# One weight transfer with eight rows a partition, a strided on-chip turn, and four transfers held back by a copy count

## The chip, the cores and the metric

The kernel runs on one core of a Trainium2 chip. A core has a matrix engine (TensorE, in the profile PE for the matrix products and PEld for its weight loads), a vector engine (VectorE, DVE), a scalar engine (ScalarE, ACT), a general engine (GpSimd, POOL) and a synchronisation engine (SyncE, SP). Each engine runs its own list of instructions and waits on counters called semaphores. Transfers between the device memory and the on-chip memory are issued by an engine and carried out by 16 DMA engines. The on-chip memory has 128 partitions.

The metric is the device time of one execution in microseconds (us). The kernel before takes 206.82 us, the median of three runs (206.81 to 207.0).

## The reference

The inputs are x of 16 x 512 x 1024, a weight of 1024 x 768, the number scale = 0.1, and add_value of 16 x 512 x 768, all in float32. What is computed is

```python
def reference(x, weight, scale, add_value):
    return (scale * np.matmul(x, weight) + add_value).astype(np.float32)
```

With the first two dimensions of x put together there are 8192 rows, contraction length K = 1024 and N = 768 columns. The kernel multiplies in bfloat16, accumulates in float32, and adds in float32.

## The kernel before, in words

The 8192 rows are cut into 64 tiles of 128 rows, numbered 0 to 63. In one group of 16 tiles, partition p holds 16 consecutive rows of the matrix, so that a transfer of eight tiles moves one contiguous run a partition: 32768 bytes of x, or 24576 bytes of add_value or of the output.

Five lists of work run side by side, one for each engine.

**SyncE** (`sync_engine`) issues nearly all transfers, in the order of the list `STREAM`. An entry names a kind, a first tile and a number of tiles: `w` is weight, `x` is the input, `a` is add_value, `o` is a store of the output, and `a+` only books the second half of a double load of add_value. The first load of x (tiles 0 to 7) is issued ahead of the list. The buffer `xs` has room for 16 tiles of x, and the buffer `ao` for 32 tiles of add_value, which also becomes the output in place. So before an entry is issued, SyncE waits for what makes its room free: for `x`, that ScalarE (`by_act`) and GpSimd (`by_pool`) have copied the tiles that it overwrites; for `a`, that the load of add_value before it has landed, and that the store that used the slots has landed; for `o`, that VectorE has finished the tiles (`made`) and that the store two before it has landed. SyncE works strictly in this order, so what stands behind a waiting entry waits too. The helper `need` leaves out a wait that an earlier one already covers. `SYNC_AT` names the place in the list at which the instruction stream is aligned; it stands before the entry `("a", 8, 8)` both times.

**ScalarE and GpSimd** (`mover`) copy x from `xs` to one of two buffers `va`, from float32 to bfloat16, four tiles at a time. Such a step of four tiles is called a move; there are 16 moves. In each move each of the two engines makes 8 copies of 32 partitions x 1024 elements, shifting blocks of 32 partitions, and each copy adds one to `by_act` or `by_pool`: after all moves each count stands at 128. Move m may start when its x has landed and when the turns of move m - 2 are done.

**VectorE** (`vector_engine`) first casts the weight to bfloat16 (`cast_w`, two instructions of four of the eight weight slabs each). Then it alternates two kinds of work. `turn` transposes 32 x 32 blocks of half a move (two tiles) from `va` to `xt`, on pairs of bfloat16 values seen as one 4-byte word. `finish` takes the products of two tiles from the accumulator `mm`, scales them and adds add_value in `ao`. Turns 0 and 1 come first; after that each finish of a pair of tiles is followed by the turn of the pair two later.

**TensorE** (`tensor_engine`) takes the tiles in order: eight weight loads a tile, and two products (512 and 256 columns) for each. It works on two tiles for each turn.

**GpSimd** also stores tiles 8 and 15 itself, as three transfers over different partitions (`BY_POOL`), after 64 of its 128 copies.

How the contraction index is dealt out matters for the change. The weight has 1024 rows. Before, slab pair c holds the rows 256 c + 2 p and 256 c + 2 p + 1 on partition p: two consecutive rows, 6144 bytes, are contiguous in the device memory, and each of the two weight transfers moves two such runs a partition. The tiles of x are put in the matching order by the copies (four runs of 64 values for each of four tiles, thus 16 x 64) and by the turn, which reads `va` from end to end.

Of the kernel before, what the change touches and what calls it, by code (L numbers as in the profile page):

```python
# [8 lines left out]
P = 128  # L9
# [7 lines left out]
VA_BUFS = 2  # L17
MOVE = 4
AHEAD = 4
HALF_BLOCK, PAST, SYNC_AT = 64, 4, 4  # L20

STREAM = [
# [6 lines left out]
]  # L29
FIRST, ENDING = (0, 8), 48  # L30
PAIR, TURN_AT = slice(8, 16, 7), 2
BY_POOL = [(122, 6), (0, 98), (98, 24)]

# [2 lines left out]
def kernel(  # L36
# [9 lines left out]
    bf16 = mybir.dt.bfloat16  # L46
    fp32 = mybir.dt.float32
# [7 lines left out]
    KC = K // (2 * P)  # L55
    KJ = 2 * KC
# [1 line left out]
    x_v = x_f.rearrange("(g p t) k -> p g t k", p=P, t=R)  # L58
    add_v = add_f.rearrange("(g p t) n -> p g t n", p=P, t=R)
    out_v = out_f.rearrange("(g p t) n -> p g t n", p=P, t=R)  # L60
    w_v = weight.rearrange("(c p r) n -> p c (r n)", p=P, r=2)

    def rows(view, s, n):
        assert s // R == (s + n - 1) // R
        return view[:, s // R, s % R:s % R + n, :]
# [3 lines left out]
    xs = nc.alloc_sbuf_tensor("xs", [P, X_SLOTS, K], fp32).ap()  # L69
    const = ctx.enter_context(tc.tile_pool(name="const", bufs=1))  # L70
    ao = const.tile([P, A_SLOTS, N], fp32, name="ao")
    w_bf = const.tile([P, KJ, N], bf16, name="w_bf")
    va = [const.tile([P, MOVE * KC, 4, 64], bf16, name=f"va{i}") for i in range(VA_BUFS)]
    xt = const.tile([P, XT_TILES, KC, P], fp32, name="xt")
    mm = psum.tile([P, MM_BUFS, 1024], fp32, name="mm")

    end_sem = nc.alloc_semaphore("ending")
    w_sem = [tc.alloc_semaphore(f"w{i}") for i in range(2)]
    x_sem = [tc.alloc_semaphore(f"x{i}") for i in range(X_SLOTS // MOVE)]
    a_sem = tc.alloc_semaphore("a")  # L80
    o_sem = [tc.alloc_semaphore(f"o{i}") for i in range(2)]
# [1 line left out]
    by_act, by_pool, pool_go, turned, casts, done, made = (  # L83
        tc.alloc_semaphore(name)
        for name in ("by_act", "by_pool", "pool_go", "turned", "casts", "done", "made"))
    TURNED = MOVE * VA_BUFS
    MADE = TURNED + 2 + MM_BUFS - 2
    W_AT = A_SLOTS - KJ

    def slot(t):  # L90
        return t % A_SLOTS
# [5 lines left out]
    def sync_engine(eng):  # L97
        groups, stores, known = 0, [], {}

        def need(sem, value):  # L100
            if known.get(sem, 0) < value:
                eng.wait_ge(sem, value)  # L102
                known[sem] = value

        for at, (op, s, n) in enumerate(STREAM):
            if at == SYNC_AT:
                eng.addr_align(HALF_BLOCK, offset=PAST, max_nops=0)
            last = s + n - 1
            if op == "w":
                dst = ao[:, W_AT + s:W_AT + s + n, :].rearrange("p (c r) n -> p c (r n)", r=2)  # L110
                move, sem = eng.dma_start(dst, w_v[:, s // 2:(s + n) // 2, :]), w_sem[s // 4]
            elif op == "x":
                k = s % X_SLOTS
                if last >= X_SLOTS:
                    moved = 8 * (last + 1 - X_SLOTS) // MOVE
                    need(by_act, moved)
                    need(by_pool, moved)
                move = eng.dma_start(xs[:, k:k + n, :], rows(x_v, s, n))  # L118
                sem = x_sem[k // MOVE]
            elif op == "a":  # L120
                if groups:
                    need(a_sem, 16 * groups)
                if last == A_SLOTS - 1:
                    need(casts, KJ)
                if s <= PAIR.start + A_SLOTS <= last:
                    need(aside_sem, 16 * len(BY_POOL))
                if s >= A_SLOTS:
                    i = next(j for j, (a, b) in enumerate(stores) if a <= last - 1 - A_SLOTS < a + b)
                    need(o_sem[i % 2], 16 * (i // 2 + 1))
                move = eng.dma_start(ao[:, slot(s):slot(s) + n, :], rows(add_v, s, n))  # L130
                sem = a_sem
                groups += 1
            elif op == "a+":
                need(a_sem, 16 * groups)
                eng.sem_inc(a_sem, 16 * (n // G - 1))
                groups += n // G - 1
                continue
            else:
                i = len(stores)
                if i > 1:  # L140
                    need(o_sem[i % 2], 16 * (i // 2))
                need(made, MADE + last + 1)
                move = eng.dma_start(rows(out_v, s, n), ao[:, slot(s):slot(s) + n, :])
                sem = o_sem[i % 2] if s < ENDING else end_sem
                stores.append((s, n))
            move.then_inc(sem, 16)
            if op == "x" and n == 2 * MOVE:
                eng.sem_inc(x_sem[k // MOVE + 1], 16)

    def mover(eng, copy, parity, count, go=None, first=0, turns=T // X_SLOTS):  # L150
        if go is None:
            eng.preload_act_table(mybir.ActivationFunctionType.Copy)  # L152
        with eng.Fori(16 * (first + 1), 16 * (first + turns) + 1, 16) as i:  # L153
            for q in range(X_SLOTS // MOVE):
                eng.wait_ge(x_sem[q], i)
                eng.wait_ge(turned, i + (4 * q - 12) if q < 3 else i)  # L156
                if go is not None:
                    eng.sem_inc(go, 1)  # L158
                k = MOVE * q
                src = xs[:, k:k + MOVE, :].rearrange("p i (c b k) -> p (i c) b k", b=4, k=64)  # L160
                for a in (parity, parity + 2):
                    for b in range(4):
                        copy(va[q % VA_BUFS][32 * b:32 * b + 32, :, a, :],  # L163
                             src[32 * a:32 * a + 32, :, b, :]).then_inc(count, 1)

    def vector_engine(eng):
        ao_g = ao.rearrange("p (g t) n -> p g t n", t=G)

        def cast_w(s, n):
            eng.wait_ge(w_sem[s // 4], 16)  # L170
            eng.tensor_copy(w_bf[:, s:s + n, :], ao[:, W_AT + s:W_AT + s + n, :]).then_inc(casts, n)  # L171

        def turn(move, half, moves=None):
            if half == 0:
                eng.wait_ge(by_act, moves)
                eng.wait_ge(by_pool, moves)  # L176
            q = 2 * half * KC
            eng.transpose(  # L178
                xt[:, 2 * half:2 * half + 2, :, :].rearrange("p i c m -> p (i c m)"),
                va[move % VA_BUFS][:, q:q + 2 * KC, :, :].bitcast(fp32).rearrange("p c a k -> p (c a k)"),  # L180
            ).then_inc(turned, 2)

        def finish(pair, at, products):
            eng.wait_ge(done, products)
            a = ao_g[:, at, 2 * pair:2 * pair + 2, :]
            q = 2 * (pair % 2)
            eng.scalar_tensor_tensor(  # L187
                a, mm[:, q:q + 2, 0:N], float(scale), a,
                op0=mybir.AluOpType.mult, op1=mybir.AluOpType.add).then_inc(made, 2)

        def group(i, at, last):
            eng.wait_ge(a_sem, i)
            for p in range(4):
                finish(p, at, i + (4 * p - 12) if p < 3 else i)
                if p < 2 or not last:
                    turn(1 if p < 2 else 0, p % 2, i + 8 if p == 2 else i)

        cast_w(0, 4)
        cast_w(4, 4)
        turn(0, 0, 8)  # L200
        turn(0, 1)
        with eng.Fori(16, 2 * T, 16) as i:
            group(i, bass.ds((i // 16 + A_SLOTS // G - 1) % (A_SLOTS // G), 1), False)
        s = slot(T - G) // G
        group(2 * T, slice(s, s + 1), True)
# [31 lines left out]
    s, n = FIRST  # L237
# [4 lines left out]
    with tc.tile_critical(no_gpsimd_drain=True):  # L242
        sync_engine(nc.sync)
        mover(nc.scalar, nc.scalar.copy, 0, by_act)
        mover(nc.gpsimd, nc.gpsimd.tensor_copy, 1, by_pool, pool_go, 0, TURN_AT)
        nc.gpsimd.wait_ge(made, MADE + PAIR.stop)
        for p, n in BY_POOL:
            store_pair(nc.gpsimd, p, n)
        nc.gpsimd.addr_align(HALF_BLOCK, offset=PAST, max_nops=0)
        mover(nc.gpsimd, nc.gpsimd.tensor_copy, 1, by_pool, pool_go, TURN_AT, T // X_SLOTS - TURN_AT)  # L250
        vector_engine(nc.vector)
        tensor_engine(nc.tensor)
# [40 lines left out]
```

## Time and profile before

| What | before |
|---|---|
| median of three runs | 206.82 us |
| the profiled execution | 206.85 us |
| its span, first to last instruction | 205.5 us |
| busy: PE, ACT, POOL, DVE | 167.5, 134.7, 137.4, 98.0 us |
| moved by the DMA engines | 87.04 MB, mean 424 GB/s |
| mean granted clock of TensorE | 0.986 |

The span is the time from the first to the last instruction of the profiled execution; 1.35 us of its 206.85 us lie around it. Rows of the trace give a start, a duration, the engine, the line in the code, the operation and, in brackets, how long the engine was idle before and what ended that. An "issue" row on SPq is the moment at which SyncE hands a transfer to the DMA engines; its landing is told as the time from issue to the last byte's completion. Windows give for a stretch of time the busy time of each engine, the granted clock, the mean busy share of the 16 DMA engines and the rate at which they moved data. That share counts a packet where it begins, so short windows can show slightly more than 1.

### The profile page before, as it was taken

How to read it: one execution, taken by the hardware profiler on the slowest of the kernel's cores; microseconds unless marked ns; L12 is line 12 of the kernel's file. 1: busy time of each engine (PE TensorE's matmuls, PEld its weight loads, DVE VectorE, ACT ScalarE, POOL GpSimd, SP SyncE). 2: the span in 40 equal slices, each digit the busy share in tenths (PEclk: the TensorE clock that was granted, in tenths of full speed). 3: DMA queues.
4: the chain of work that ended last, by engine and by line, in shares of the span. 5: the costliest groups of instructions: out<-in, count | busy, mean ns of one | idle time of the engine just before them, and what ended most of it. 6: DMA issues, size and time to landing. Idle time of an engine off the chain costs nothing.

```text
span 205.5 us, 2223 instructions
## 1 busy us (share of the span) xinstructions
PE 167.5 (82%) x1008; PEld 50.4 (25%) x512; DVE 98.0 (48%) x66; ACT 134.7 (66%) x129; POOL 137.4 (67%) x135
## 2 busy tenths in 40 slices
PE   0000099999999999999999999999999997999900
PEld 0000022233322333223332233332333322333200
DVE  0004525537555555465555555555552853455330
ACT  2049980699999906999999059999991099920000
POOL 0049994699999916999999549999992099930000
PEclk9999999999999999999999999999999999999995
DMA  8989999999999899999999999999999999998997
GB/s 287 427 372 438 440 485 408 392 437 459 446 459 459 357 459 408 408 426 413 455 404 450 431 416 464 434 411 421 440 431 415 437 448 421 493 459 364 423 440 304
DMA packets 4065, 87.04 MB, mean 424 GB/s; under 512 B 480, under 2 KB 480, under 8 KB 1120
## 3 DMA queue, kind: packets, MB, share of 16 engines
q1 hardware_dynamic: 3856, 86.25, 98.1%
q0 software_dynamic: 208, 0.79, 0.9%
q14 instruction: 1, 0.01, 0.0%
HBM read 61.87 MB, written 25.17 MB: 424 GB/s over the span
## 4 chain that ended last, share of the span: by engine, by line
DMA 38%; PE 36%; POOL 10%; ACT 5%; issue 4%; DVE 3%; SPq 1%; POOLq 0%; DVEq 0%; ACTq 0%
PE mm L210 36%; DMA out_dram<-ao 22%; DMA xs<-in_x_dram 15%; POOL va L163 9%; ACT va L163 5%; DVE xt L178 2%; DVE ao L187 1%; POOL out_dram L95 1%; SPq L130 0%; SPq L118 0%; DVEq L176 0%; SPq L102 0%; POOLq L156 0%; POOLq L158 0%; POOLq L153 0%
## 5 line engine op out<-in xcount | busy, mean ns | idle before, releaser
L210 PE MATMUL mm<-w_bf,xt 128*128 128x256 bf16 (+1 forms) x1008 | 167.5, 327 | 28.0 <-DVE xt L178 27.1
L163 POOL CAST va<-xs 32x1024 bf16<-32x1024 f32 x128 | 135.2, 1056 | 44.2 <-DMA xs<-in_x_dram 36.8
L163 ACT CAST va<-xs 32x1024 bf16<-32x1024 f32 x128 | 133.4, 1042 | 45.2 <-DMA xs<-in_x_dram 42.2
L187 DVE SCALAR_TENSOR_TENSOR ao<-mm,ao 128x1536 f32 (+1 forms) x32 | 56.2, 1756 | 72.9 <-PE mm L210 68.9
L208 PEld LDWEIGHTS <-xt 128*128 128x128 bf16 x512 | 50.4, 98 | 144.6 <-issue 116.6
L178 DVE STREAM_TRANSPOSE xt<-va 128x1024 f32<-128x1024 f32 x32 | 39.4, 1234 | 8.4 <-POOL va L163 6.3
L171 DVE CAST w_bf<-ao 128x3072 bf16<-128x3072 f32 x2 | 4.5, 2240 | 18.1 <-DMA ao<-in_weight_dram 18.1
L152 ACT ACT_TABLE_LOAD x1 | 1.3, 1283 | 1.3 <-SPq L242 1.3
L95 POOL DMA_DIRECT2D out_dram<-ao x3 | 2.0, 672 | 0.0
L274 POOL MEMSET const-float32-0.0<- 128x1 f32 x1 | 0.1, 98 | 0.2 <-issue 0.2
L274 POOL MEMSET const-bfloat16-1.0<- 128x1 bf16 x1 | 0.1, 101 | 0.0
L274 POOL MEMSET const-float32-1.0<- 128x1 f32 x1 | 0.1, 98 | 0.0
L274 POOL MEMSET const-uint8-127<- 128x1 uint8 x1 | 0.1, 98 | 0.0
## 6 DMA issues: line engine op xcount, KB each, us to landing
xs<-in_x_dram SPq DMA_DIRECT2D x7, 4096.0 KB, 20.9
ao<-in_add_value_dram SPq DMA_DIRECT2D x6, 3072.0 KB, 15.7
out_dram<-ao SPq DMA_DIRECT2D x3, 3072.0 KB, 27.4
ao<-in_add_value_dram SPq DMA_DIRECT2D x1, 6144.0 KB, 24.2
out_dram<-ao SPq DMA_DIRECT2D x1, 6144.0 KB, 31.2
out_dram<-ao SPq DMA_DIRECT2D x1, 4608.0 KB, 14.9
xs<-in_x_dram SPq DMA_DIRECT2D x2, 2048.0 KB, 21.0
ao<-in_weight_dram SPq DMA_DIRECT2D x2, 1536.0 KB, 16.8
```

The lines of the kernel that those rows point to most:

```text
L95: eng.dma_start(out_v[p:p + n, 0, PAIR, :], ao[p:p + n, PAIR, :]).then_inc(aside_sem, 16)
L152: eng.preload_act_table(mybir.ActivationFunctionType.Copy)
L163: copy(va[q % VA_BUFS][32 * b:32 * b + 32, :, a, :], src[32 * a:32 * a + 32, :, b, :]).then_inc(count, 1)
L171: eng.tensor_copy(w_bf[:, s:s + n, :], ao[:, W_AT + s:W_AT + s + n, :]).then_inc(casts, n)
L178: eng.transpose(xt[:, 2 * half:2 * half + 2, :, :].rearrange("p i c m -> p (i c m)"), va[move % VA_BUFS][:, q:q + 2 * KC, :, :].bitcast(fp ...
L187: eng.scalar_tensor_tensor(a, mm[:, q:q + 2, 0:N], float(scale), a, op0=mybir.AluOpType.mult, op1=mybir.AluOpType.add).then_inc(made, 2)
L208: eng.ldweights(x_j, tile_position=(0, 0))
L210: m = eng.add_instruction(mybir.InstMatmult(start_tensor_calc=(j == 0), stop_tensor_calc=(j == KJ - 1), tile_size=(P, P), tile_position=(0 ...
L274: nc = _bacc.Bacc("TRN2", target_bir_lowering=False, num_devices=1)
```

## The change

There are three edits.

1. The weight comes in one transfer. Partition p now gets the eight consecutive rows 8 p to 8 p + 7, which is one run of 24576 bytes. There is one semaphore for it, so both casts wait for the whole weight. SyncE issues one transfer less. `SYNC_AT` goes from 4 to 3, since the list is shorter by one.
2. The order of x has to follow. The copies now move four runs of 256 consecutive values (4 x 256 in place of 16 x 64, still 1024 elements). The turn reads `va` with a step of four 4-byte words between neighbouring elements and writes `xt` from end to end as before.
3. A table `HELD` adds a wait on ScalarE's count `by_act` ahead of four entries of the list: the store of tile 0 on (54 copies), the load of add_value for tile 32 on (66), the store of tile 16 on (92) and the store of tile 32 on (119). What follows such an entry in the list is issued behind it, as always.

```diff
-HALF_BLOCK, PAST, SYNC_AT = 64, 4, 4
+HALF_BLOCK, PAST, SYNC_AT = 64, 4, 3
 STREAM = [
-    ("w", 0, 4), ("w", 4, 4), ("a", 0, 8),
+    ("w", 0, 8), ("a", 0, 8),
     ("x", 8, 8), ("a", 8, 8), ("x", 16, 8), ("a", 16, 16), ("x", 24, 8),
     ("x", 32, 8), ("a+", 16, 16), ("o", 0, 8), ("o", 9, 6), ("a", 32, 8), ("x", 40, 8),
     ("a", 40, 8), ("x", 48, 8), ("o", 16, 8), ("o", 24, 8), ("a", 48, 8), ("x", 56, 4),
...
+HELD = {("o", 0): 54, ("a", 32): 66, ("o", 16): 92, ("o", 32): 119}
...
-    w_v = weight.rearrange("(c p r) n -> p c (r n)", p=P, r=2)
+    w_v = weight.rearrange("(p r) n -> p r n", r=KJ)
...
-    va = [const.tile([P, MOVE * KC, 4, 64], bf16, name=f"va{i}") for i in range(VA_BUFS)]
+    va = [const.tile([P, MOVE, 4, 2 * P], bf16, name=f"va{i}") for i in range(VA_BUFS)]
...
-    w_sem = [tc.alloc_semaphore(f"w{i}") for i in range(2)]
+    w_sem = tc.alloc_semaphore("w")
...
+            if (op, s) in HELD:
+                need(by_act, HELD[op, s])
             if op == "w":
-                dst = ao[:, W_AT + s:W_AT + s + n, :].rearrange("p (c r) n -> p c (r n)", r=2)
-                move, sem = eng.dma_start(dst, w_v[:, s // 2:(s + n) // 2, :]), w_sem[s // 4]
+                move, sem = eng.dma_start(ao[:, W_AT + s:W_AT + s + n, :], w_v[:, s:s + n, :]), w_sem
...
-                src = xs[:, k:k + MOVE, :].rearrange("p i (c b k) -> p (i c) b k", b=4, k=64)
+                src = xs[:, k:k + MOVE, :].rearrange("p i (b k) -> p i b k", b=4)
...
-            eng.wait_ge(w_sem[s // 4], 16)
+            eng.wait_ge(w_sem, 16)
...
-            q = 2 * half * KC
+            i = slice(2 * half, 2 * half + 2)
             eng.transpose(
-                xt[:, 2 * half:2 * half + 2, :, :].rearrange("p i c m -> p (i c m)"),
-                va[move % VA_BUFS][:, q:q + 2 * KC, :, :].bitcast(fp32).rearrange("p c a k -> p (c a k)"),
+                xt[:, i, :, :].rearrange("p i c (a m) -> p i c a m", a=4),
+                va[move % VA_BUFS][:, i, :, :].bitcast(fp32).rearrange("p i a (k c) -> p i c a k", c=KC),
             ).then_inc(turned, 2)
```

## The prediction

> **What bounds the kernel now.** I read the page first: the span, the engines' busy time, the DMA digits and queues.
>
> ```profile
> span 205.5 us, 2223 instructions
> PE 167.5 (82%) x1008; PEld 50.4 (25%) x512; DVE 98.0 (48%) x66; ACT 134.7 (66%) x129; POOL 137.4 (67%) x135
> DMA  8989999999999899999999999999999999998997
> q1 hardware_dynamic: 3856, 86.25, 98.1%
> q0 software_dynamic: 208, 0.79, 0.9%
> ```
>
> Packets occupy the 16 DMA engines for 98.1% + 0.9% = 99.0% of the span, TensorE is at 82%. Windows show where the missing percent lies (columns: stretch, length, busy time of PE, PEld, DVE, ACT, POOL, clock, DMA share, GB/s).
>
> ```profile
> 0.00:1.70 1.70, 0.00 (x0) 0.00 (x0) 0.00 (x0) 0.36 (x1) 0.20 (x4) 1.00 0.00 0
> 1.70:12.00 10.30, 0.00 (x0) 0.00 (x0) 0.00 (x0) 0.93 (x1) 0.00 (x0) 1.00 1.01 407
> 12.00:204.00 192.00, 167.51 (x1008) 50.38 (x512) 97.97 (x66) 133.43 (x128) 137.16 (x131) 0.99 1.00 431
> 204.00:205.50 1.50, 0.00 (x0) 0.00 (x0) 0.00 (x0) 0.00 (x0) 0.00 (x0) 0.50 0.24 98
> ```
>
> From 12 to 204 us the share is 1.00 at 431 GB/s. The time is therefore: 1.7 us before the first byte, the packets, about 1 us at the end. A change helps only if the packets take less time, and hurts only if it makes the queue run dry or makes the last store late by more than the queue ahead of it lasts. Everything below is measured against these two conditions.
>
> **Part 1, the weight in one transfer.** The landings at the start can be read off who waited for them: ScalarE starts when x 0 to 7 landed, the casts when a weight half landed, SyncE's issue at 27.64 when the first add_value landed.
>
> ```profile
> 0.74 0.38 SPq L239 DMA_DIRECT2D xs<-in_x_dram  x1
> 12.89 17.04 ACT L163 CAST va<-xs 32x1024 bf16<-32x1024 f32 x16 [10.26 <-DMA xs<-in_x_dram]
> 13.04 20.27 POOL L163 CAST va<-xs 32x1024 bf16<-32x1024 f32 x16 [12.60 <-DMA xs<-in_x_dram]
> 16.65 2.31 DVE L171 CAST w_bf<-ao 128x3072 bf16<-128x3072 f32 x1 [16.65 <-DMA ao<-in_weight_dram]
> 20.40 2.17 DVE L171 CAST w_bf<-ao 128x3072 bf16<-128x3072 f32 x1 [1.44 <-DMA ao<-in_weight_dram]
> 24.69 2.37 DVE L178 STREAM_TRANSPOSE xt<-va 128x1024 f32<-128x1024 f32 x2 [2.12 <-ACT va L163]
> 27.64 0.33 SPq L130 DMA_DIRECT2D ao<-in_add_value_dram  x1
> ```
>
> The weight (3072 KB in 6144-byte runs) took 20.40 - 12.89 = 7.51 us of queue time. The load behind it, also 3072 KB but in 24576-byte runs, took 27.64 - 20.40 = 7.24 us. The changed weight load has exactly that second shape, so I take 7.24: a gain of 0.27 us. Bounds: 0, if the difference belonged to the stage and not to the runs, and 0.27. Because the queue stays full, what is saved moves every later packet forward; I take 0.25.
>
> A page's rule says otherwise. The Trainium skill, SBUF — State Buffer, section "The DMA setup-cost knee", gives every transfer a roughly fixed 2 us; one transfer fewer would then be an estimated 2 us. The rows do not bear that out: the second half landed 20.40 - 16.65 = 3.75 us after the first, and 1536 KB at the 431 GB/s of the long window takes 3.65 us. At most 0.1 us a transfer was visible.
>
> The casts both wait now. With the weight landed at 20.40 - 0.27 = 20.13, they run back to back for 2.31 + 2.17 = 4.48 us, until 24.61, and the first turn would start at about 24.7; before it started at 24.69, since it waited for copies. (16 GpSimd copies took 20.27 us beside the casts; the wait is named after ScalarE, but ScalarE's eighth copy was done by about 12.89 + 17.04/2 = 21.4, so GpSimd's eighth is the likelier one, and it is as long beside the casts wherever they stand.) So TensorE starts at the old 26.0 plus what the first turn gains or loses. One issue of about 0.45 us less on SyncE lies in front of transfers that queue for over 10 us: nothing.
>
> **Part 2, the copies and the strided turn.** A copy keeps its 1024 elements, 32 partitions and engine, in longer runs; I take its time, 1035 ns on GpSimd and 17.04/16 = 1.065 us a step on ScalarE, as unchanged. The turn's stride of four words appears nowhere in this trace.
>
> ```profile
> L163 POOL CAST va<-xs x16: 1026/1035/2452, 13.0 to 32.3; 32x1024 bf16<-32x1024 f32 x16
> L178 DVE STREAM_TRANSPOSE xt<-va x32: 1202/1233/1246, 24.7 to 186.8; 128x1024 f32<-128x1024 f32 x32
> L171 DVE CAST w_bf<-ao x2: 2167/2240/2314, 16.7 to 20.4; 128x3072 bf16<-128x3072 f32 x2
> 64.31 1.76 DVE L187 SCALAR_TENSOR_TENSOR ao<-mm,ao 128x1536 f32 x1 [2.29 <-PE mm L210]
> 65.98 1.23 DVE L178 STREAM_TRANSPOSE xt<-va 128x1024 f32<-128x1024 f32 x1
> 69.51 1.76 DVE L187 SCALAR_TENSOR_TENSOR ao<-mm,ao 128x1536 f32 x1 [2.29 <-PE mm L210]
> ```
>
> Lower bound: VectorE's fastest rate here, 2240 ns for 3072 elements, gives 0.75 us, a gain of 0.48. Upper bound: the only row in which one operation took much longer than its like is the GpSimd copy, 2452 against 1035 ns; that ratio of 2.37 gives 1.233 x 2.37 = 2.92 us, a loss of 1.69. The nearest row is the turn itself, 1.23 us for the same elements, at a rate of 1.2 ns an element that is slower than VectorE's other rows, so that there may be room for the reads; I take 1.23.
>
> Both ends are covered in the steady state: a pair of tiles takes 69.51 - 64.31 = 5.20 us, of which VectorE idles 2.29, so a turn may grow by 2.2 us, to about 3.4, before TensorE waits. At the end the copies wait for x 56 to 59, and the turn behind them is exposed once:
>
> ```profile
> 173.19 1.26 DVE xt L178
> 174.49 20.97 PE L210 MATMUL mm<-w_bf,xt 128*128 128x512 bf16 x126 [1.13 <-DVE xt L178]
> 195.57 1.76 DVE L187 SCALAR_TENSOR_TENSOR ao<-mm,ao 128x1536 f32<-128x1536 f32 x1 [3.44 <-PE mm L210]
> 186.96 10.78 SPq L143 DMA_DIRECT2D out_dram<-ao  x2
> 197.41 0.33 SPq L143 DMA_DIRECT2D out_dram<-ao  x1
> out_dram<-ao SPq DMA_DIRECT2D x1, 4608.0 KB, 14.9
> ```
>
> The last store is issued at 197.41, while the store before it, issued at 186.96, lands at 201.86. An issue into an empty queue needed 0.74 to 1.7 us = 1.0 us to the first byte and then lost 10.30 x (431 - 407)/431 = 0.6 us until the flow was full. Allowing about 1.5 us for the receipt of the last bytes and for engines that run dry earlier than others, the last store may come 201.86 - 1.5 - 1.6 - 197.41 = 1.3 us later for nothing. So a turn up to about 2.5 us costs nothing, one of 2.92 us costs 0.4.
>
> The Trainium skill, SBUF — State Buffer, section "Specifications (TRN2)", speaks against this edit: on-chip memory is read in 16-byte lines, full bandwidth needs at least two hits a line, and every crossing costs. The new turn touches each line once. A halved rate would be an estimated 2.47 us a turn, at the edge of what is free.
>
> **Part 3, the four holds.** The copies' groups give the release times (a copy is due every 34.12/32 = 1.066 us), the issues, each with the time to landing of its transfer below it, tell what is still queued then (of the two stores from 73.13 on, the second, issued at about 73.5).
>
> ```profile
> 78.70 34.12 ACT L163 CAST va<-xs 32x1024 bf16<-32x1024 f32 x32 [7.14 <-DMA xs<-in_x_dram]
> 120.55 34.12 ACT L163 CAST va<-xs 32x1024 bf16<-32x1024 f32 x32 [7.73 <-DMA xs<-in_x_dram]
> 164.23 17.04 ACT L163 CAST va<-xs 32x1024 bf16<-32x1024 f32 x16 [9.56 <-DMA xs<-in_x_dram]
> 72.62 0.33 SPq L118 DMA_DIRECT2D xs<-in_x_dram  x1
> xs<-in_x_dram SPq DMA_DIRECT2D x1, 4096.0 KB, 16.0
> 73.13 0.82 SPq L143 DMA_DIRECT2D out_dram<-ao  x2
> out_dram<-ao SPq DMA_DIRECT2D x1, 2304.0 KB, 28.2
> 116.82 0.39 SPq L118 DMA_DIRECT2D xs<-in_x_dram  x1
> xs<-in_x_dram SPq DMA_DIRECT2D x1, 4096.0 KB, 20.6
> 159.26 0.33 SPq L130 DMA_DIRECT2D ao<-in_add_value_dram  x1
> ao<-in_add_value_dram SPq DMA_DIRECT2D x1, 3072.0 KB, 17.1
> ```
>
> Those groups begin with copies 49, 81 and 113. Store 0 goes from 73.13 to 78.70 + 6 x 1.066 = 85.1; x 32 (issued 72.62) lands at 88.6: 3.5 us ahead. Load 32 goes to 78.70 + 18 x 1.066 = 97.9; the store of tiles 9 to 14 lands at 101.7: 3.8 ahead. Store 16 goes to 120.55 + 12 x 1.066 = 133.3; x 48 (issued 116.82) lands at 137.4: 4.1 ahead. Store 32 goes to 164.23 + 7 x 1.066 = 171.7; load 56 (issued 159.26) lands at 176.4: 4.7 ahead. Needed are the same 1.5 + 1.6 = 3.1 us. All four clear it, the first by only 0.4. Behind the held entries wait, in order, the store of 9 to 14, x 40, store 24, and store 48; none is due before the queue has emptied, and none of the counts waits for anything queued behind its own hold (copy 54 needs x 24, issued earlier, and so on). The x loads keep their places, because the queue serves in the order of issue. Cost: 0; bounds: 0.15 us gained (below) to some 4 us lost (four dry spells of 1.0).
>
> **Sum**: 206.85 - 0.25 + 0 + 0 = 206.6 us for the profiled execution, which is 0.03 above the median of 206.82; I predict 206.6. A difference of 0.2% (0.41 us) is about what a measurement can tell from none.
>
> **Rivals.**
> - *Holds quiet the changeover from loads to stores.* One window in the middle is slow, just where the first store follows x 32:
>
> ```profile
> 86.00:88.00 2.00, 1.95 (x13) 0.64 (x7) 1.20 (x2) 1.95 (x3) 1.88 (x3) 1.00 1.04 397
> ```
>
>   Share full, 397 GB/s: 2 x (431 - 397)/431 = 0.15 us. If a store queued behind a load slows it, the hold gives that back, and something smaller at three more places, say 0.3 together: 206.85 - 0.25 - 0.3 = 206.3. Against it: the other changeovers show no such window. Chance 0.27.
> - *The fixed cost of a transfer goes*: 204.8, against the 0.1 us seen. Chance 0.02.
> - *A hold starves the queue* (the other side). Place: the issue of store 0, the thinnest margin. It decides once an issue needs over 3.5 us of lead in place of 3.1. A dry spell of 1.0 us at one hold gives 207.6, at all four 210.6. Chance 0.13.
> - *The turn is slow.* At 2.92 us: 207.0; beyond 3.4 us VectorE sets the pace, and a turn of 3.7 us makes a pair last 0.3 us longer, 31 times over: some 9 us, of which the end's slack takes 1.3. Chance 0.1, raised from 0.06 by the line rule above.
>
> **Chances.** The forecast has 0.48. Faster 0.29 (first two rivals), same 0.49 (the forecast and a little of the turn), slower 0.22. The likeliest case alone spans 206.45 to 206.9 (weight gain 0 to 0.27, scatter of 0.1). With the changeover rival and one dry spell: 206.1 to 207.8.
>
> **What would show it.** The two casts back to back from about 20.1; add_value landing about 0.25 earlier; packets fewer by 384 (3072 KB in runs of 6144 bytes are 512, of 24576 bytes 128); DMA share still 1.00 in the long window. Store 0 issued near 85, load 32 near 98, store 16 near 133, store 32 near 171.5. The turn's mean in its row decides part 2. I am wrong if a window after 85, 98, 133 or 171 shows a share well under 1.00, if PE idles over the 1.1 us before the last 126 products, or if 86 to 88 us goes up to 430 GB/s and the total falls by more than 0.4.

## The result and the profile after

The changed kernel takes 207.96 us in the median (206.79 to 209.5), the kernel before 206.83 us (206.67 to 207.41). The ratio is 1.0057, 95% interval 1.0041 to 1.0072: slower by 0.57%, where 206.6 us, 0.1% faster, was forecast. The scatter belongs to the result: the runs of the changed kernel spread over 2.7 us, those of the kernel before over 0.7. The profiled execution took 207.31 us (206.85 before), so it shows less than half of the median's loss.

The page of the changed kernel: span, busy time, DMA share in 40 slices, the packets and the queue, the row of the turn.

```profile
span 206.0 us, 2223 instructions
PE 167.7 (81%) x1008; PEld 50.4 (24%) x512; DVE 123.6 (60%) x66; ACT 134.7 (65%) x129; POOL 137.4 (67%) x135
DMA  7999999999999999999999999999999999999996
DMA packets 3665, 87.04 MB, mean 423 GB/s; under 512 B 464, under 2 KB 464, under 8 KB 592
q1 hardware_dynamic: 3456, 86.25, 97.7%
L180 DVE STREAM_TRANSPOSE xt<-va 128x1024 f32<-128x1024 f32 x32 | 65.2, 2040 | 2.4 <-POOL va L165 2.3
```

SyncE's queue and VectorE's start, from the timeline of the changed kernel:

```profile
20.29 4.59 DVE L173 CAST w_bf<-ao 128x3072 bf16<-128x3072 f32 x2 [20.29 <-DMA ao<-in_weight_dram]
24.79 3.90 DVE L180 STREAM_TRANSPOSE xt<-va 128x1024 f32<-128x1024 f32 x2
27.51 0.33 SPq L132 DMA_DIRECT2D ao<-in_add_value_dram  x1
84.97 0.82 SPq L145 DMA_DIRECT2D out_dram<-ao  x2
97.78 0.34 SPq L132 DMA_DIRECT2D ao<-in_add_value_dram  x1
133.38 0.82 SPq L145 DMA_DIRECT2D out_dram<-ao  x2
171.90 26.82 SPq L145 DMA_DIRECT2D out_dram<-ao  x3
198.39 0.33 SPq L145 DMA_DIRECT2D out_dram<-ao  x1
```

The four holds let go where the copies' count puts them. The packets are fewer by 400 (4065 before): 384 from the weight, 16 tiny ones. A turn takes 2.04 us instead of 1.23. None of this looks like a loss. The loss shows only in narrow windows. The kernel before, windows at the first changeover to stores, at the next one, and at the very end (columns as in the prediction; the last two are the DMA share and GB/s):

```profile
84.00:88.00 4.00, 3.95 (x25) 1.23 (x13) 2.09 (x2) 3.90 (x5) 3.76 (x5) 1.00 1.04 420
99.00:102.00 3.00, 3.00 (x20) 0.95 (x10) 1.29 (x1) 2.95 (x3) 2.82 (x4) 1.00 1.03 440
204.00:205.00 1.00, 0.00 (x0) 0.00 (x0) 0.00 (x0) 0.00 (x0) 0.00 (x0) 0.50 0.35 148
205.00:206.00 1.00, 0.00 (x0) 0.00 (x0) 0.00 (x0) 0.00 (x0) 0.00 (x0) 0.50 0.00 0
```

The changed kernel, the same windows and the long one:

```profile
12.00:204.00 192.00, 167.65 (x1008) 50.38 (x512) 123.61 (x66) 133.47 (x128) 137.17 (x131) 0.99 1.00 431
84.00:88.00 4.00, 4.00 (x27) 1.22 (x13) 2.52 (x3) 3.93 (x4) 3.76 (x5) 1.00 0.86 369
99.00:102.00 3.00, 2.95 (x19) 0.95 (x10) 1.69 (x2) 2.95 (x3) 2.82 (x4) 1.00 1.00 373
204.00:205.00 1.00, 0.00 (x0) 0.00 (x0) 0.00 (x0) 0.00 (x0) 0.00 (x0) 0.50 0.30 123
205.00:206.00 1.00, 0.00 (x0) 0.00 (x0) 0.00 (x0) 0.00 (x0) 0.00 (x0) 0.50 0.03 12
```

The long window is as full as before: 1.00 at 431 GB/s. But at 99 to 102 us the full engines move 373 GB/s instead of 440, and after 205 us there is still a share of 0.03, one packet of one DMA engine, while the others are done. These windows need care: they count a packet where it begins, and one packet of 32768 bytes takes 1.2 us, so a window of a few microseconds can be off by a good part. With the bytes of each packet spread over its duration, 99 to 102 us comes to 380 GB/s against 428. At 84 to 88 us it comes to 431 against 406, so there the changed kernel is not slow at all, although its row says 0.86 and 369.

The same can be worked out from the packet records, which give start, duration and bytes of each packet. By them an engine is idle for 0.08 us between 20 and 200 us, before and after the change, so there is no dry spell. In the table the first column is the sum of all packet times over 16, without the packets of a few bytes; the ends are those of the last packet of each DMA engine. (The records don't name the engine; a packet was linked to the one that ended just before it.)

```
                      sum/16   median end   last three ends
before                203.30     204.66     204.91 204.91 205.00
changed               203.05     204.38     204.98 205.09 205.61
```

The work fell by 0.25 us, of which the weight's own packets are 0.20 (7.50 to 7.30 us). The middle engine finished 0.28 us earlier. The last one finished 0.61 us later, and the last one sets the time.

### The profile page after: what moved, and what is told of

It reads as the page before. It is cut to its first block, busy times and chain, and to the rows that moved or that the text cites. A ratio compares the mean times of both kernels' runs of the same rounds, so it can differ in the third digit from the quotient of the medians.

```text
span 206.0 us, 2223 instructions
## 1 busy us (share of the span) xinstructions
PE 167.7 (81%) x1008; PEld 50.4 (24%) x512; DVE 123.6 (60%) x66; ACT 134.7 (65%) x129; POOL 137.4 (67%) x135
## 4 chain that ended last, share of the span: by engine, by line
PE 56%; DMA 18%; POOL 12%; issue 5%; DVE 4%; SPq 0%; DVEq 0%; POOLq 0%
PE mm L212 56%; POOL va L165 12%; DMA xs<-in_x_dram 9%; DMA ao<-in_weight_dram 9%; DVE xt L180 2%; DVE ao L189 1%; DVE w_bf L173 1%; SPq L241 0%; DVEq L204 0%; POOLq L158 0%; POOLq L155 0%; DVEq L189 0%; DVEq L178 0%; POOLq L160 0%; SPq L257 0%
## 5 line engine op out<-in xcount | busy, mean ns | idle before, releaser
L180 DVE STREAM_TRANSPOSE xt<-va 128x1024 f32<-128x1024 f32 x32 | 65.2, 2040 | 2.4 <-POOL va L165 2.3
```

What stands on the lines that cost most here:

```text
L180: eng.transpose(xt[:, i, :, :].rearrange("p i c (a m) -> p i c a m", a=4), va[move % VA_BUFS][:, i, :, :].bitcast(fp32).rearrange("p i a ( ...
```

## The experiments

**The holds, or the rest?** Two kernels divide the change in two, two more the part without holds. First the changed kernel without holds:

```diff
-HELD = {("o", 0): 54, ("a", 32): 66, ("o", 16): 92, ("o", 32): 119}
+HELD = {}
```

> The changed kernel without the four holds (HELD empty); the weight in one transfer and the strided turn stay. Theory H (the holds issue four transfers too shortly ahead of the moment at which the DMA engines need them, and single engines lose time at the changeovers): 206.6 us, ratio 0.998 to 1.000, with the narrow scatter of the kernel before. Rival T (the turn, 2.04 us in place of 1.23, makes the last store 1 us late): as slow as the changed kernel, ratio 1.004 to 1.007. Rival W (the weight in one transfer): the same as T.

Measured 207.03 us (206.79 to 207.2), ratio 0.9999 (0.9990 to 1.0008).

Then the kernel before with the same table `HELD` and its two lines in `sync_engine`:

> The kernel before with the four holds alone. H: the whole loss, ratio 1.004 to 1.007, with runs spread over 2 us. T and W: ratio 1.000.

Measured 208.63 us (206.9 to 210.19), ratio 1.0075 (1.0052 to 1.0098). The holds carry the whole loss and the whole scatter; the turn and the weight together cost nothing. T and W fall. That the last store goes out later is no cause either: without holds it was issued at 198.57, in the changed kernel at 198.39.

The weight alone (the kernel before with `("w", 0, 8)`, one semaphore, and the new view of the weight):

```diff
-    w_v = weight.rearrange("(c p r) n -> p c (r n)", p=P, r=2)
+    w_v = weight.rearrange("(p r) n -> p r n", r=KJ)
```

> The kernel before with the weight in one transfer of eight rows a partition, and nothing else: the copies and the turn keep the old order of x, so the products pair other rows of the weight with x and the output is not the reference's; the work is the same in size. H and T: 0.25 us faster, ratio 0.9985 to 0.9995, since the packets of the weight take less time. W: ratio 1.004 or more.

Measured 206.99 us (206.83 to 207.93), ratio 1.0004 (0.9994 to 1.0013): no gain, where 0.25 us was expected.

The turn alone (the changed kernel, no holds, the weight as `("w", 0, 4), ("w", 4, 4)` with two semaphores):

> The strided turn alone: the changed kernel without holds and with the weight in two transfers of four rows a partition (runs of 12288 bytes). T: ratio 1.004 or more. H and W: ratio 0.999 to 1.001, the turn's 0.8 us hidden behind the DMA queue.

Measured 206.91 us (206.74 to 207.1), ratio 0.9996 (0.9987 to 1.0005). The turn's extra 0.8 us is hidden, as forecast.

**Where the weight's 0.25 us stayed.** With the weight alone it arrived early: the casts start at 20.14, and SyncE's next issue, which waits for the first add_value, comes at 27.34 instead of 27.64. In the changed kernel without holds that head start is missing (20.41 and 27.63), because the first load of x landed 0.2 us later in that execution (ScalarE starts at 13.11 instead of 12.89). Two windows of its profile:

```profile
84.00:88.00 4.00, 4.00 (x26) 1.18 (x12) 2.55 (x2) 3.90 (x5) 3.76 (x5) 1.00 0.83 270
205.00:206.00 1.00, 0.00 (x0) 0.00 (x0) 0.00 (x0) 0.00 (x0) 0.00 (x0) 0.50 0.00 0
```

From 84 to 88 us the row has 270 GB/s, the kernel before 420; with the packets spread over their durations it is 349 against 406. Call extra time what packets take beyond the usual for their size, averaged over the 16 engines. From 84 to 88 us it was 0.81 us here and 0.84 with the weight alone; it was 0.25 in the kernel before and 0.47 with the turn alone. The stretch at the first changeover took back what the weight had saved. All three profiles with the weight in one transfer and store 0 issued early have 0.75 to 0.84, the eleven with the weight in two transfers 0.13 to 0.57. Why the stretch is longer with one transfer wasn't separated.

**Which hold?** The kernel before with one entry of `HELD` at a time.

> The kernel before with one hold alone, store 0 on 54 copies. Theory L (what a hold costs depends on how long before the DMA engines' need it lets the issue go; leads between the issue and the landing of the transfer ahead: 3.5 us at store 0, 3.8 at load 32, 4.1 at store 16, 4.7 at store 32): the largest of the four, ratio 1.003 to 1.005. Rival C (store 0 queued for 12 us behind a load disturbs that load, the slow window at 86 us; holding it gives this back): ratio 0.998 to 0.9995. Rival E (every hold costs alike, about a quarter of the loss): 1.001 to 1.002.

Measured 209.04 us (207.24 to 209.55), ratio 1.0087 (1.0065 to 1.0108).

> The kernel before with the hold of load 32 on 66 copies alone; two copies, 2 us, later than before. L: 1.001 to 1.003. C: 1.000. E: 1.001 to 1.002.

Measured 208.1 us (207.29 to 208.37), ratio 1.0045 (1.0028 to 1.0062).

> The kernel before with the hold of store 16 on 92 copies alone. L: 1.001 to 1.002. E: 1.001 to 1.002. A fourth account, by the packets' skew in the profiles with holds (single engines late at 148 and 174 us): this one and store 32 carry the loss, 1.003 or more each.

Measured 207.04 us (206.87 to 207.44), ratio 0.9998 (0.9982 to 1.0014).

> The kernel before with the hold of store 32 on 119 copies alone. L: the smallest, 1.000 to 1.001. E: 1.001 to 1.002. By the skew: 1.003 or more.

Measured 207.02 us (206.84 to 207.35), ratio 0.9995 (0.9979 to 1.0011).

The lead of a hold is the time from the late issue to the landing of the transfer in front of it. The order is that of the leads: 3.5 us costs most, 3.8 half of that, 4.1 and 4.7 nothing. (Leads are reckoned here, as in the prediction, with the landings of the kernel before. In the kernel that holds load 32 the store in front landed at 102.39 instead of 101.74, so a few tenths between two places mean little.) The costs don't add up: store 0 alone costs 0.87%, all four together 0.75%, and the two intervals overlap. Equal shares (E) and the account by skew at 148 and 174 us fall. The hold of store 0 alone shows most clearly what happens:

```profile
84.00:88.00 4.00, 4.00 (x26) 1.18 (x12) 2.05 (x2) 3.90 (x5) 3.76 (x5) 1.00 1.03 442
99.00:102.00 3.00, 3.00 (x20) 0.88 (x9) 0.83 (x2) 2.92 (x4) 2.82 (x4) 1.00 1.04 416
205.00:206.00 1.00, 0.00 (x0) 0.00 (x0) 0.00 (x0) 0.00 (x0) 0.00 (x0) 0.50 0.09 37
206.00:207.00 1.00, 0.00 (x0) 0.00 (x0) 0.00 (x0) 0.00 (x0) 0.00 (x0) 0.50 0.03 12
```

The slow stretch at 84 to 88 us is gone (442 GB/s), as my rival C had it, and the time is still the worst of the four. There is no dry spell at 87 us either. The disturbance turns up 13 us later, around 99.6 us, where the queue goes from the store of tiles 9 to 14 to load 32; GpSimd's first packets follow only at 101.39. In the packet records one packet there takes 907 ns more than its kind, and from that load on the latest engine stays about 1.1 us behind the next: the ends are 205.11, 205.58 and 206.78, with the sum over 16 at 203.56. For the last 1.7 us two of the 16 engines at most are still at work. The hold of load 32 gives the same picture (one packet 1082 ns longer at 101.3 us; ends 204.95, 206.21, 206.23).

**Lead, or GpSimd's stores?** Two accounts were left: the lead by itself, and the meeting with GpSimd's stores. First the kernel before without those stores: the entry `("o", 9, 6)` becomes `("o", 8, 8)`, `store_pair` is not called, and load 40 doesn't wait for it.

> The kernel before, with tiles 8 and 15 stored by SyncE in one store of tiles 8 to 15, and GpSimd storing nothing. It is the base for the next two. All theories: 0.998 to 1.004, with no late engine around 100 us.

Measured 208.18 us (207.88 to 208.45), ratio 1.0055 (1.0042 to 1.0068).

> As the one before, with the hold of store 0 on 54 copies, which alone cost 0.9%. Theory G (a hold costs because GpSimd's stores meet the queue in another state near 100 us, and one DMA engine falls a microsecond behind): the same time as without the hold, within 0.1%. Theory L (3.5 us of lead are too little for any engine): 0.5 to 1% slower than without the hold.

Measured 208.03 us (207.77 to 208.6), ratio 1.0052 (1.0039 to 1.0065): 0.07% under the run without the hold.

> As the first, with the hold of load 32 on 66 copies, which alone cost 0.45%. G: within 0.1% of the run without the hold. L: 0.3 to 0.5% slower than it.

Measured 208.31 us (207.93 to 208.54), ratio 1.0057 (1.0044 to 1.0070): 0.06% over it.

So without GpSimd's stores the hold of store 0 costs nothing more. But the base is already slow: its profile has one engine far behind (ends 204.92, 205.09, 206.06, median 204.50), and a hold's late engine can hide beside one that is late anyway. The trace says that it does: with the hold of store 0 three engines are late (205.84, 206.01, 206.10). From 95 to 104 us the extra time is 0.17 us with this hold and 0.03 without, one packet at 101.2 us taking 827 ns too long, though GpSimd stores nothing. The disturbance doesn't need those stores, so the equal times don't speak for theory G.

The run with load 32 held says little. The store in front of it now carries eight tiles and lands at 103.45 in the run without holds; load 32 is issued at 98.03, so the lead is 5.4 us and not 3.8.

GpSimd's rows may be dealt unevenly in such a way that the engines come out level; a pair of runs further down tries that. First, the lead alone:

```diff
-HELD = {("o", 0): 54}
+HELD = {("o", 0): 50}
```

> The kernel before with store 0 held for 50 copies in place of 54: issued at 78.70 + 2 x 1.066 = 80.8 us, 7.8 us ahead of the landing of the load in front of it, over twice the lead. L: ratio 0.999 to 1.001. G: still slower, 1.004 to 1.009, since the issue still falls after 73 and the state at 100 us is shifted.

Measured 206.94 us (206.79 to 207.16), ratio 0.9996 (0.9988 to 1.0005). L holds here and G alone does not: a hold with 7.8 us of lead is free.

**How much lead?** The same with 52 and with 56 copies, load 32 with one copy less, and the changed kernel with three of its holds released four copies earlier and load 32 not held.

> The kernel before with store 0 held for 52 copies: issued at about 83.0 us, 5.6 us ahead of the landing of the load in front of it (50 copies, 7.8 us: no cost; 54 copies, 3.5 us: 0.9%). Theory L (the lead decides, with a threshold): 1.000 if the threshold lies below 5.6, in any case between 1.000 and 1.009. Rival D (no order in it; each shift of an issue throws the 16 DMA engines' balance another way): anything, also above 1.009.

Measured 207.03 us (206.8 to 207.24), ratio 1.0001 (0.9992 to 1.0011).

> The kernel before with store 0 held for 56 copies: issued at about 87.3 us, 1.4 us ahead. L: more than the 0.9% of 54 copies, 1.01 or above, with a DMA share visibly under 1.00 around 88 us. D: anything, also 1.000.

Measured 209.73 us (209.69 to 209.94), ratio 1.0135 (1.0119 to 1.0150).

> The kernel before with load 32 held for 65 copies: issued at about 96.8 us, 4.9 us ahead of the landing of the store in front of it (unheld: 96.0; 66 copies: 97.9 and 0.45%). L: 1.000 to 1.002. D: anything. A third account (the load has to come ahead of GpSimd's three stores, issued from 96.2 to 98.3): like 66 copies, 1.003 to 1.006.

Measured 207.0 us (206.8 to 207.39), ratio 1.0001 (0.9992 to 1.0010).

> The changed kernel with the holds of stores 0, 16 and 32 released four copies earlier (50, 88, 115) and load 32 not held. L: 0.999 to 1.001, like the changed kernel without holds. D: 1.003 or more.

Measured 207.08 us (206.79 to 207.41), ratio 1.0005 (0.9995 to 1.0014). Leads of 7.8 and 5.6 us at store 0 are free, 3.5 costs 0.9%, 1.4 costs 1.35%; 4.9 at load 32 is free, 3.8 costs 0.45%. D falls: with longer leads each shift is harmless. The third account falls in part. At 65 copies load 32 was issued at 96.81, behind the first of GpSimd's three stores and ahead of the other two, and that was free; at 66 copies it came behind all three. So at load 32 the lead and the order aren't separated; at store 0, where load 32 stayed ahead of all three, only the lead changed. The changed kernel is cured by releasing three holds four copies earlier and dropping the fourth, and is then as fast as the kernel before; no kernel here was faster than that one beyond its interval.

The packet records join the lead to the disturbance. Over all twenty profiles the extra time from 95 to 104 us is 0.12 to 1.03 us in the seven kernels with a lead of 3.8 us or less, and 0.02 to 0.05 in the thirteen others.

Only at 56 copies does the queue run dry, in the profile of that kernel:

```profile
86.00:88.00 2.00, 2.00 (x14) 0.59 (x7) 1.84 (x2) 1.95 (x3) 1.88 (x3) 1.00 0.61 262
99.00:102.00 3.00, 3.00 (x20) 0.91 (x10) 0.83 (x2) 2.93 (x4) 2.82 (x4) 1.00 0.98 283
207.00:208.00 1.00, 0.00 (x0) 0.00 (x0) 0.00 (x0) 0.00 (x0) 0.00 (x0) 0.50 0.06 25
```

Store 0 was issued at 87.31 and its first packet starts at 88.16, 0.85 us later. The idle time comes to 0.57 us a DMA engine, by the packet records. More is lost at 99 to 102 us, 283 GB/s (the 1.03 us of extra time just named), and one engine is again 1.4 us behind the next at the end (206.59 and 208.04).

**Are the engines kept level by GpSimd's rows?**

```diff
-BY_POOL = [(122, 6), (0, 98), (98, 24)]
+BY_POOL = [(0, 98), (98, 24), (122, 6)]
```

> The kernel before with GpSimd's three stores in another order (98 rows, 24 rows, 6 rows in place of 6, 98, 24): the same bytes, dealt to other DMA engines. Theory B (the end is set by the latest of 16 DMA engines, and the uneven rows of these stores level one that is late anyway, which is why the kernel without them takes 0.55% longer): 1.003 to 1.008. Without B: 1.000.

Measured 208.34 us (208.19 to 208.43), ratio 1.0060 (1.0047 to 1.0073). Its ends: median 204.62, last three 204.79, 205.07, 206.48, the sum over 16 unchanged at 203.33.

> The same with store 0 held for 54 copies. B: within 0.3% of the run without the hold, at either side, since which engine is late changes. If the hold costs by itself: 0.9% slower than the run without it.

Measured 209.18 us (208.19 to 209.99), ratio 1.0095 (1.0072 to 1.0119); 0.40% over the run without the hold. This last one is inconclusive: it lies between the two expectations. The one before is not: the same bytes in another order cost 0.6%, and in the profile one engine ends 1.4 us after the next.

```profile
205.00:206.00 1.00, 0.00 (x0) 0.00 (x0) 0.00 (x0) 0.00 (x0) 0.00 (x0) 0.50 0.06 25
206.00:207.00 1.00, 0.00 (x0) 0.00 (x0) 0.00 (x0) 0.00 (x0) 0.00 (x0) 0.50 0.03 12
```

That fits theory B but doesn't show it, for this engine falls behind late. When x 48 is done, at 137 us, the last engine is 0.43 us behind the middle one (0.38 in the kernel before); at 159 us it is 0.91 and at 192 us 1.58 behind, while GpSimd's last store landed at 116.39. The kernel without GpSimd's stores looks alike: 0.30, 0.80 and 1.28. What holds this engine up after 137 us wasn't found, and neither kernel has the disturbance at 95 to 104 us (0.02 and 0.03).

## Why the prediction was wrong, point by point

- **The bound** was read rightly, and the conclusion from it wrongly. The step that failed is the sentence that a change "hurts only if it makes the queue run dry or makes the last store late by more than the queue ahead of it lasts". There is a third way: one of 16 engines falls behind while all stay busy. The mean share that I read, 1.00 before and after, can't show that.
- **Part 3** is where this entered the sum. "Needed are the same 1.5 + 1.6 = 3.1 us" sized the lead against dryness. Against dryness it was ample: 1.4 us was dry, 3.5 was not. In the dry kernel the first byte came 0.85 us after the issue, where I had 1.0 and 0.6 more to fill up, and the first engine ran out 1.05 us before the landing (87.33 and 88.38), where I had allowed 1.5. But the cost sets in with more lead: 3.8 us costs, 4.9 at the same transfer and 4.1 at another don't. The term "Cost: 0" measured 208.63 - 206.92 = 1.7 us with the holds alone and 207.96 - 206.83 = 1.1 in the changed kernel, inside the bounds of a gain of 0.15 to a loss of 4, and its upper end was built on dry spells that didn't occur. The release times were right within 0.2 us (84.97, 97.78, 133.38, 171.90).
- **The rival on the other side** had the right place (store 0, the thinnest margin). That its 207.6 for one spell lies near the 207.96 measured is luck, since no engine ran dry. The changeover rival was right that a held store quiets 84 to 88 us, 442 against 420 GB/s; it missed that the disturbance comes back at 99 us and there hits single engines.
- **Part 1**: the weight's packets became shorter by 0.20 us, where I took 0.25. That what is saved "moves every later packet forward" failed: with the weight alone the ratio is 1.0004, and its profile shows add_value 0.30 us earlier and the gain lost at 84 to 88 us. The casts came as forecast, at 20.29 for 20.13, and the turn at 24.79 for 24.7. The Trainium skill's fixed 2 us a transfer (SBUF — State Buffer, section "The DMA setup-cost knee") is not seen in these runs: a transfer fewer in a full queue gained nothing.
- **Part 2**: the turn was sized wrongly, 2.04 us where I took 1.23, inside the bounds of 0.75 and 2.92. The Trainium skill's rule on 16-byte lines (SBUF — State Buffer, section "Specifications (TRN2)") had the direction: the step of one line an element costs a factor of 1.65, not the 2 of my estimate. That up to 2.5 us would cost nothing was right: TensorE started 0.8 us later, the last store was issued at 198.39 instead of 197.41, and the turn alone measured 0.9996.

What stays open: why a transfer issued less than about 4 us ahead stretches packets some 12 us further on and leaves one or two engines late, when no engine ran dry. The runs show that at store 0 the lead decides, and the traces that the stretched packets come with the short leads; the mechanism between the two was not seen. That GpSimd's rows keep the engines even, and that this evenness is what the holds upset, is argued and not shown. The kernel without those rows and the one with another order have a late engine of their own, which arises elsewhere.

## What to carry to other kernels

When the DMA share is 1.00, look at the spread of the last packets' ends and not only at the sum: one engine of 16 sets the time, and 0.25 us of saved work can stand beside 0.6 us of delay. A transfer that has to follow on without a gap was free here at every lead tried from 4.1 us up (4.1, 4.7, 4.9, 5.6, 7.8); holding it to 3.8 us or less brought nothing and cost the kernel before 0.45 to 1.35%. The places differ, so 4 us is no sharp limit. Such a loss hides in a mean over the engines; it shows in the windows after the last bulk transfer and in a wider scatter of the runs.

## What had not been expected of the hardware

- The order of three small stores (0.79 MB of 87) moves the time by 0.6%; one DMA engine then ends 1.4 us after the next. Why is open.
- A 32 x 32 block transpose of 1024 4-byte elements takes 2.04 us when neighbours are read 16 bytes apart, 1.23 us when they lie side by side.
- Where the first store follows a load, the packets in flight, fully busy engines, take up to 0.8 us longer each engine (349 GB/s against 431 in a kernel whose store is held). Holding the store to 85 us moves the disturbance 13 us later, onto single engines, instead of removing it.
